# An 8192 x 8192 fp32 transpose: all stores, and all loads but the first three, issued by ScalarE instead of SyncE, with the stores ahead of the load

## The chip, the cores and the metric

One core of one Trainium2 chip. The metric is the device time of one execution, in microseconds (us), lower is better.

A ratio below is the mean time of one kernel's runs over the mean of the runs of the kernel before in the same rounds, so it is not quite the ratio of the medians quoted beside it. It comes with a 95% interval.

## The reference

```python
def setup_inputs():
    return {"x": np.random.randn(8192, 8192).astype(np.float32)}

def reference(x):
    return np.transpose(x)
```

268 MB go in and 268 MB come out; nothing is computed.

## The kernel before

The matrix is walked in 128 chunks of 128 rows by 4096 columns (2 MB). SyncE loads a chunk into one of NIN = 3 input buffers. TensorE, in a hardware loop, transposes it into the eight banks of PSUM (the memory that TensorE writes), 512 columns each. ScalarE copies the even banks and VectorE the odd banks into output registers: big buffers that gather the same bank over a window of up to 8 chunks, so that a store writes 4 KB runs. One bank closes its window in each chunk and SyncE stores that register (2 MB). There are nine registers: eight with open windows and one spare. So a window that opens in chunk t reuses the register whose store was issued in chunk t-2, and the copying engine waits for it.

```python
        def load(t):
            s, c = chunks[t]
            nc.sync.dma_start(
                out=ins[t % NIN], in_=x[c * P:(c + 1) * P, s * J:(s + 1) * J]
            ).then_inc(s_ld[t % NIN], 16)
        # ...
        for t, (s, c) in enumerate(chunks):
            closing = []
            for q in range(NR):
                e = q % 2
                eng = (nc.scalar, nc.vector)[e]
                if q not in window:
                    # ... take a register r, open a window
                    if stored[r]:
                        eng.wait_ge(s_st[r], 16 * stored[r])
                # ...
                eng.wait_ge(s_pe, t * NR + q + 1)
                # ... copy pss[q] into its place in regs[r]
            if t + NIN < T:
                nc.sync.wait_ge(s_pe, (t + 1) * NR)     # TensorE is done with chunk t
                load(t + NIN)
            for q, e, count in closing:
                nc.sync.wait_ge(s_cp[e], count)         # the last copy of the window
                # ... store regs[r] on SyncE's queue
```

Of the kernel before, what the change touches and what calls it, by code (L numbers as in the profile page):

```python
# [8 lines left out]
def physical(ap):  # L9


    t = ap.tensor
    dims = [list(d) for d in ap.ap]
    if len(dims) == 2:
        dims.insert(1, [dims[1][1], 1])
    return mybir.PhysicalAccessPattern(
        ap=dims,
        offset=ap.offset,
        dtype=ap.dtype,
        memref=t.name,  # L20
        memsetref=t.name + "_set",
    )


def wide_dma(nc, eng, queue, out, in_):


    return eng.add_instruction(
        mybir.InstDMACopy(
            mode="Copy",  # L30
            name=nc.get_next_instruction_name(),
            engine=eng.engine,
            ins=[physical(in_)],
            outs=[physical(out)],
            queue=queue,
        )
    )


@with_exitstack  # L40
def kernel(
    ctx: ExitStack,
    tc: tile.TileContext,
    x: bass.AP,
    out: bass.AP,
):






    nc = tc.nc
    P = 128
    N, M = x.shape
    assert x.shape == out.shape[::-1]
    dt = x.dtype

    S = 32
    B = 4  # L60
    W = 8
    NR = S // B
    NIN = 3
    NREG = 9
    CH = N // P
    J = S * P

    with tc.tile_critical():  # L68
        nc.alloc_sbuf_tensor("pad", [P, 32], dt)
        ident = nc.alloc_sbuf_tensor("ident", [P, P], dt).ap()  # L70
        ins = [nc.alloc_sbuf_tensor(f"in{k}", [P, J], dt).ap() for k in range(NIN)]
        regs = [nc.alloc_sbuf_tensor(f"reg{k}", [P, B * W * P], dt).ap() for k in range(NREG)]
        pss = [nc.alloc_psum_tensor(f"ps{k}", [P, B * P], dt).ap() for k in range(NR)]

        s_id = nc.alloc_semaphore("s_id")
        s_ld = [nc.alloc_semaphore(f"s_ld{k}") for k in range(NIN)]
        s_st = [nc.alloc_semaphore(f"s_st{k}") for k in range(NREG)]
        s_bank = [nc.alloc_semaphore(f"s_bank{q}") for q in range(NR)]
        s_pe = nc.alloc_semaphore("s_pe")
        s_cp = [nc.alloc_semaphore("s_cpa"), nc.alloc_semaphore("s_cpv")]  # L80

        nc.gpsimd.memset(ident, 0.0).then_inc(s_id, 1)  # L82
        nc.gpsimd.wait_ge(s_id, 1)
        nc.gpsimd.affine_select(  # L84
            out=ident,
            in_=ident,
            compare_op=mybir.AluOpType.not_equal,
            fill=1.0,
            base=0,
            pattern=[[-1, P]],  # L90
            channel_multiplier=1,
        ).then_inc(s_id, 1)

        chunks = [(s, c) for s in range(M // J) for c in range(CH)]

        def load(t):
            s, c = chunks[t]
            nc.sync.dma_start(
                out=ins[t % NIN], in_=x[c * P:(c + 1) * P, s * J:(s + 1) * J]
            ).then_inc(s_ld[t % NIN], 16)  # L100




        def transposes(t):
            k = t % NIN
            nc.tensor.sem_inc(s_ld[k], -16).wait_op(s_ld[k], 16, "sem-ge")
            for q in range(NR):
                if t:
                    nc.tensor.sem_inc(s_bank[q], -1).wait_op(s_bank[q], 1, "sem-ge")  # L110
                for b in range(B):
                    tr = nc.tensor.transpose(  # L112
                        pss[q][:, b * P:(b + 1) * P],
                        ins[k][:, q * B * P + b:(q + 1) * B * P - B + b + 1:B],
                        ident,
                    )
                    if b == B - 1:
                        tr.then_inc(s_pe, 1)

        T = len(chunks)  # L120
        nc.tensor.wait_ge(s_id, 2)
        for t in range(T % NIN):
            transposes(t)
        with nc.Fori(0, T // NIN, engines=[nc.tensor.engine]):
            for t in range(NIN):
                transposes(T % NIN + t)

        for t in range(NIN):
            load(t)

        copied = [0, 0]
        free = list(range(NREG))
        stored = [0] * NREG
        window = {}
        stores = 0

        def closes(w, t):
            t0, r, parts = w
            return t + 1 == t0 + sum(z - a for _, a, z in parts)
# [10 lines that stand above are left out]
                    span = (q - c) % W + 1  # L150
                    r = free.pop(0)
                    parts = [(s, c, min(c + span, CH))]
                    if c + span > CH and t + span < T:
                        parts.append((s + 1, 0, c + span - CH))
                    window[q] = (t, r, parts)
                    if stored[r]:
                        eng.wait_ge(s_st[r], 16 * stored[r])
                t0, r, parts = window[q]
                k = [p[0] for p in parts].index(s)
                base = B * P * sum(z - a for _, a, z in parts[:k])  # L160
                _, a, z = parts[k]
                view = regs[r][:, base:base + B * (z - a) * P].rearrange("p (b i) -> p b i", b=B)
                o = view[:, :, (c - a) * P:(c - a + 1) * P]
                i = pss[q].rearrange("p (b i) -> p b i", b=B)
                eng.wait_ge(s_pe, t * NR + q + 1)
                if e == 0:
                    cp = nc.scalar.copy(out=o, in_=i)  # L167
                else:
                    cp = nc.vector.tensor_copy(out=o, in_=i)  # L169
                if closes(window[q], t):  # L170
                    cp.then_inc(s_cp[e], 1)
                    copied[e] += 1
                    closing.append((q, e, copied[e]))
                    eng.wait_ge(s_cp[e], copied[e])
                    eng.sem_inc(s_bank[q], 1)
                else:
                    cp.then_inc(s_bank[q], 1)
            if t + NIN < T:
                nc.sync.wait_ge(s_pe, (t + 1) * NR)
                load(t + NIN)  # L180
            for q, e, count in closing:
                t0, r, parts = window.pop(q)
                nc.sync.wait_ge(s_cp[e], count)
                base = 0
                for s_, a, z in parts:
                    rows = (z - a) * P
                    j0 = s_ * J + q * B * P
                    dst = out[j0:j0 + B * P, a * P:a * P + rows]
                    dst = dst.rearrange("(q b) i -> q b i", q=P)
                    src = regs[r][:, base:base + B * rows]  # L190
                    base += B * rows
                    if stores:
                        st = wide_dma(nc, nc.sync, "qSPDynamicHW", dst, src)
                    else:
                        st = nc.sync.dma_start(
                            out=dst, in_=src.rearrange("q (b i) -> q b i", b=B)
                        )
                    st.then_inc(s_st[r], 16)
                    stores += 1
                    stored[r] += 1  # L200
                free.append(r)
        for r in range(NREG):
            nc.sync.wait_ge(s_st[r], 16 * stored[r])

# [29 lines left out]
```

## Time and profile before

| | |
|---|---|
| time, median of 3 | 1267.63 us (1267.36 to 1267.84) |
| span in the profile | 1264.3 us |
| moved | 536.89 MB in the one queue, 99.8% of the span |
| TensorE / VectorE / ScalarE busy | 718.0 / 330.8 / 278.2 us |
| load, full store: issue to landing | 19.5 us, 24.3 us |

The page's lines and their reading are in the prediction. In all such lines PE is TensorE, DVE VectorE and ACT ScalarE; SPq and ACTq are issues of transfers by SyncE and by ScalarE, and "landing" is the moment when a transfer is complete. One more view, the waits (engine, line, what it waited for: total us, times, longest):

```profile
ACT reg L167 <- DMA out_dram<-reg: 787.7, 63, 17.7
DVE reg L169 <- DMA out_dram<-reg: 746.3, 63, 17.0
```

Together 1534.0 us of standing until a store has landed.

### The profile page before, as it was taken

To read this page: it belongs to the slowest core of one execution; us is meant where nothing else is said; L and a number is where in the kernel's file an instruction comes from. 1 tells how busy PE (TensorE), PEld (TensorE's weight loads), DVE (VectorE), ACT (ScalarE), POOL (GpSimd) and SP (SyncE) were. 2 spreads that over 40 slices of the span, in tenths; PEclk is the share of its full clock that TensorE was granted. 3 is DMA by queue.
4 is the path that set the end of the run, shared out by engine and by line. 5 is a ranking of instruction groups with operands and counts; after the bars stand their busy time and mean duration, and the time that the engine had idled before them with its cause. 6 is when DMAs were issued, how large, how long until landed. Compare 5 with 4: busy or idle time off the path is not lost. (4 is left out here: it accounts for less than half of the span.)

```text
span 1264.3 us, 11043 instructions
## 1 busy us (share of the span) xinstructions
PE 718.0 (57%) x4096; PEld 679.5 (54%) x4096; DVE 330.8 (26%) x512; ACT 278.2 (22%) x513; POOL 0.7 (0%) x6
## 2 busy tenths in 40 slices
PE   5746566465565646655565564655647555565560
PEld 5646466454555546555564554655546555465550
DVE  3312213222232222221222212222122222232220
ACT  2322132121321212213122121221312213122130
POOL 0000000000000000000000000000000000000000
PEclk9977867787876877767678777887777868778785
DMA  9999999999999999999999999999999999999997
GB/s 384 428 429 429 429 429 429 429 430 429 429 430 429 429 430 430 430 430 429 430 423 417 431 430 429 430 428 431 430 428 429 430 430 431 428 429 430 429 429 308
DMA packets 39277, 537.00 MB, mean 425 GB/s; under 512 B 4320, under 2 KB 4832, under 8 KB 6240
## 3 DMA queue, kind: packets, MB, share of 16 engines
q1 hardware_dynamic: 39264, 536.89, 99.8%
q14 instruction: 12, 0.10, 0.0%
q8 instruction: 1, 0.02, 0.0%
HBM read 268.44 MB, written 268.44 MB: 425 GB/s over the span
## 5 line engine op out<-in xcount | busy, mean ns | idle before, releaser
L112 PE MATMUL ps<-ident,in 128*128 128x128 f32 x4096 | 718.0, 351 | 516.0 <-PEq L110 506.9
L112 PEld LDWEIGHTS ps<-ident,in 128*128 128x128 f32 x4096 | 679.5, 218 | 554.1 <-issue 552.9
L169 DVE COPY reg<-ps 128x512 f32<-128x512 f32 x512 | 330.8, 686 | 904.5 <-DMA out_dram<-reg 746.3
L167 ACT COPY reg<-ps 128x512 f32<-128x512 f32 x512 | 276.9, 596 | 957.4 <-DMA out_dram<-reg 787.7
L167 ACT ACT_TABLE_LOAD x1 | 1.3, 1283 | 0.9 <-SPq L68 0.9
L84 POOL TENSOR_SCALAR_AFFINE_SELECT ident<-ident 128x128 f32<-128x128 f32 x1 | 0.3, 292 | 0.2 <-POOL ident L82 0.2
L82 POOL MEMSET ident<- 128x128 f32 x1 | 0.2, 205 | 0.5 <-SPq L68 0.5
L218 POOL MEMSET const-bfloat16-1.0<- 128x1 bf16 x1 | 0.1, 101 | 0.0
L218 POOL MEMSET const-uint8-127<- 128x1 uint8 x1 | 0.1, 101 | 0.0
L218 POOL MEMSET const-float32-0.0<- 128x1 f32 x1 | 0.1, 98 | 0.2 <-issue 0.2
L218 POOL MEMSET const-float32-1.0<- 128x1 f32 x1 | 0.1, 98 | 0.0
## 6 DMA issues: line engine op xcount, KB each, us to landing
in<-in_x_dram SPq DMA_DIRECT2D x128, 2048.0 KB, 19.5
out_dram<-reg SPq DMA_DIRECT2D x114, 2048.0 KB, 24.3
out_dram<-reg SPq DMA_DIRECT2D x4, 1792.0 KB, 22.6
out_dram<-reg SPq DMA_DIRECT2D x4, 1536.0 KB, 21.3
out_dram<-reg SPq DMA_DIRECT2D x4, 1280.0 KB, 18.1
out_dram<-reg SPq DMA_DIRECT2D x4, 1024.0 KB, 19.1
out_dram<-reg SPq DMA_DIRECT2D x4, 768.0 KB, 18.8
out_dram<-reg SPq DMA_DIRECT2D x4, 512.0 KB, 17.2
```

The costliest lines, as they stand in the source:

```text
L82: nc.gpsimd.memset(ident, 0.0).then_inc(s_id, 1)
L84: nc.gpsimd.affine_select(out=ident, in_=ident, compare_op=mybir.AluOpType.not_equal, fill=1.0, base=0, pattern=[[-1, P]], channel_multipl ...
L112: tr = nc.tensor.transpose(pss[q][:, b * P:(b + 1) * P], ins[k][:, q * B * P + b:(q + 1) * B * P - B + b + 1:B], ident,)
L167: cp = nc.scalar.copy(out=o, in_=i)
L169: cp = nc.vector.tensor_copy(out=o, in_=i)
L218: nc = _bacc.Bacc("TRN2", target_bir_lowering=False, num_devices=1)
```

## The change

The intent is to free SyncE of nearly its whole program. ScalarE issues all stores and all loads but the first three, on its own queue. With it the order changes: the stores of a chunk go out from inside the row of ScalarE's copies, the load after the last copy. TensorE's loop is the same in both kernels.

```diff
-            nc.sync.dma_start(
+            (nc.sync if t < NIN else nc.scalar).dma_start(
                 out=ins[t % NIN], in_=x[c * P:(c + 1) * P, s * J:(s + 1) * J]
...
+        def store(q, e, count):
+            t0, r, parts = window.pop(q)
+            nc.scalar.wait_ge(s_cp[e], count)
...
+                    st = wide_dma(nc, nc.scalar, "qActDynamicHW", dst, src)
...
+                before = []
+                if e == 0:
+                    before, closing = closing, []
                 if closes(window[q], t):
...
+                for k in before:
+                    store(*k)
+            for k in closing:
+                store(*k)
             if t + NIN < T:
-                nc.sync.wait_ge(s_pe, (t + 1) * NR)
+                nc.scalar.wait_ge(s_pe, (t + 1) * NR)
                 load(t + NIN)
-            for q, e, count in closing:
...
-                    st = wide_dma(nc, nc.sync, "qSPDynamicHW", dst, src)
```

More of the change, by code (lines that the diff above doesn't have):

```diff
@@ L134 @@
         window = {}
-        stores = 0
+        def store(q, e, count):
+            t0, r, parts = window.pop(q)
+            nc.scalar.wait_ge(s_cp[e], count)
+            base = 0
+            for s, a, z in parts:
+                rows = (z - a) * P
+                j0 = s * J + q * B * P
+                dst = out[j0:j0 + B * P, a * P:a * P + rows]
+                dst = dst.rearrange("(q b) i -> q b i", q=P)
+                src = regs[r][:, base:base + B * rows]
+                base += B * rows
+                if any(stored):
+                    st = wide_dma(nc, nc.scalar, "qActDynamicHW", dst, src)
+                else:
+                    st = nc.scalar.dma_start(
+                        out=dst, in_=src.rearrange("q (b i) -> q b i", b=B)
+                    )
+                st.then_inc(s_st[r], 16)
+                stored[r] += 1
+            free.append(r)
         def closes(w, t):
@@ L177 @@
                     cp.then_inc(s_bank[q], 1)
+                for k in before:
+                    store(*k)
+            for k in closing:
+                store(*k)
             if t + NIN < T:
-                nc.sync.wait_ge(s_pe, (t + 1) * NR)
+                nc.scalar.wait_ge(s_pe, (t + 1) * NR)
                 load(t + NIN)
-            for q, e, count in closing:
-                t0, r, parts = window.pop(q)
-                nc.sync.wait_ge(s_cp[e], count)
-                base = 0
-                for s_, a, z in parts:
-                    rows = (z - a) * P
-                    j0 = s_ * J + q * B * P
-                    dst = out[j0:j0 + B * P, a * P:a * P + rows]
-                    dst = dst.rearrange("(q b) i -> q b i", q=P)
-                    src = regs[r][:, base:base + B * rows]
-                    base += B * rows
-                    if stores:
-                        st = wide_dma(nc, nc.sync, "qSPDynamicHW", dst, src)
-                    else:
-                        st = nc.sync.dma_start(
-                            out=dst, in_=src.rearrange("q (b i) -> q b i", b=B)
-                        )
-                    st.then_inc(s_st[r], 16)
-                    stores += 1
-                    stored[r] += 1
-                free.append(r)
         for r in range(NREG):
```

## The prediction

> **What bounds the kernel now.** I read the page first: engines, slices, queues, groups, DMA issues.
>
> ```profile
> PE 718.0 (57%) x4096; PEld 679.5 (54%) x4096; DVE 330.8 (26%) x512; ACT 278.2 (22%) x513; POOL 0.7 (0%) x6
> ...
> DMA  9999999999999999999999999999999999999997
> GB/s 384 428 429 429 429 429 429 429 430 429 429 430 429 429 430 430 430 430 429 430 423 417 431 430 429 430 428 431 430 428 429 430 430 431 428 429 430 429 429 308
> ...
> q1 hardware_dynamic: 39264, 536.89, 99.8%
> ...
> L169 DVE COPY reg<-ps 128x512 f32<-128x512 f32 x512 | 330.8, 686 | 904.5 <-DMA out_dram<-reg 746.3
> L167 ACT COPY reg<-ps 128x512 f32<-128x512 f32 x512 | 276.9, 596 | 957.4 <-DMA out_dram<-reg 787.7
> ...
> in<-in_x_dram SPq DMA_DIRECT2D x128, 2048.0 KB, 19.5
> out_dram<-reg SPq DMA_DIRECT2D x114, 2048.0 KB, 24.3
> ```
>
> No engine is busy over 57%. One DMA queue is busy 99.8% of the span, flat at about 429.5 GB/s. ScalarE and VectorE spend most of their idle time waiting for a store to land, so the transfers lead and the engines follow. Moving 536.89 MB at 429.5 GB/s takes 1250.0 us. The span is 1264.3, and the page says where the other 14 us are: a slice is 31.6 us, the first (384) loses 31.6 x (1 - 384/429.5) = 3.3 us, the slices with 423 and 417 lose 1.4, the last (308) loses 8.9; together 13.6. The time as measured, 1267.6, is 3.3 above the span.
>
> Next the SyncE timeline, because its work is what moves. An undisturbed chunk in the middle of the run, and the stretch where stores are cut in two because a window crosses from one half of the columns to the other:
>
> ```profile
> 508.30 0.33 SPq L98 DMA_DIRECT2D in<-in_x_dram  x1
> ...
> 508.67 0.55 SPq L28 DMA_DIRECT2D out_dram<-reg  x1
> ```
>
> ```profile
> 646.23 0.89 SPq L98 DMA_DIRECT2D in<-in_x_dram  x1
> 647.16 2.55 SPq L28 DMA_DIRECT2D out_dram<-reg  x2
> 655.35 0.99 SPq L98 DMA_DIRECT2D in<-in_x_dram  x1
> 656.39 3.34 SPq L28 DMA_DIRECT2D out_dram<-reg  x2
> ...
> 672.81 3.26 SPq L98 DMA_DIRECT2D in<-in_x_dram  x1
> 676.12 2.71 SPq L28 DMA_DIRECT2D out_dram<-reg  x2
> ```
>
> A load costs its issuer 0.33 us and a store 0.55 us, while landing takes some 20 us. In the split stretch an issue can take 3.3 us: there the issuer is held back, I take it because the queue has no room. That hold is the one thing that could hurt on an engine that also copies.
>
> **What the Trainium skill says.** "DMA: Bandwidth & Descriptors", section "Issuing engines are not separate DMA queues": transfers started by the scalar, sync or gpsimd engine run on the same 16 DMA engines, and a choice of issuer saves only the sequencer's initiating time. The trace of before has one queue only, so it shows only the second half: 0.33 to 0.55 us of issue against about 20 us to landing. The same page, section "Where 436 GB/s comes from", puts the ceiling at 435.2 GB/s; this trace runs at 429.5, 1.3% below, so a different issuer has nothing left to win there. "Perfetto Trace Analysis", section "DMA Instruction — HWDGE (DVE, Sync)": the record of such an instruction covers waiting for the generator, generating descriptors and excess semaphore increments, then the sequencer is free. The 0.33 us for a 2 MB load, which needs 4.9 us at 429.5 GB/s, agrees.
>
> **The change part by part.** A period is one chunk: 2 MB in and 2 MB out, 2 x 2.097/0.4295 = 9.77 us; call it P, and one transfer 4.88.
>
> Removed: SyncE's 125 later loads, 142 stores and their waits. SyncE was never on the chain for long, so removing it is worth nothing by itself.
>
> Added to ScalarE: 125 x 0.33 = 41 us of loads, 142 x 0.55 = 78 us of stores. The holds: over the two medians the split stretch shows about 21 us (for example 3.26 - 0.33 for the load at 672.81), and the last seven stores, which the timeline has as one run to the end, about 16 more. Together about 156 us. With 278 us of copies ScalarE is occupied 434 us, 34% of the span, and 957 us were idle. Per ordinary chunk that is 4 x 0.60 of copies plus 0.88 of issue, 3.3 us of 9.77. Room enough; what counts is whether an issue comes too late for the queue.
>
> Moved: SyncE sent load t+3 when TensorE had finished chunk t, then store t. Now store t goes first, from inside the row of copies, and load t+3 goes after ScalarE's last copy of chunk t. And ScalarE waits: the bank whose window closed in chunk t-1 opens a new window in chunk t, in the register stored at t-2, so every second chunk ScalarE stands still until store t-2 has landed, with issues behind it. Is the queue empty by then?
>
> First test the reckoning on before. With the queue always full and each load ahead of its store, put the landing of load t+3 at time 0. Load t landed at -29.3, store t-3 at -29.3 + 4.88 = -24.4, store t-2 at -14.7. TensorE needs the bank that waited for store t-3, about -23.8 with one copy, and finishes the chunk some 4 us later, near -19.7. So load t+3 should land 19.7 us after issue and store t 4.88 - 0.37 later in the queue than that, 24.2. The page has 19.5 and 24.3. The reckoning holds.
>
> Now the changed order, store t landing at 0 and load t+3 at 4.88. Load t landed at 4.88 - 29.3 = -24.4; store t-2 at -19.5. TensorE takes 718/128 = 5.6 us, from -24.4 to -18.8, no longer held by a bank (store t-3 landed at -29.3). Odd t: ScalarE stands until -19.5, then has up to four copies (2.4 us) and a store issue (0.55); store t goes out at about -18, load t+3 at about -16.5. Even t: VectorE is the one that stands; the store goes out between -22 and -18.5, the load near -18. A transfer must be in the queue 4.88 before it lands, so the spare time is at least 18 - 4.88 = 13 us for stores, and 16.5 + 4.88 - 4.88 = 16.5 us for loads. Before it was 24.3 - 4.88 = 19.4 and 19.5 - 4.88 = 14.6. The smallest margin falls from 14.6 to 13 us: still over two transfers. Nothing of ScalarE's added 156 us is on the path.
>
> Start: loads 0 to 2 stay on SyncE. Load 3 was issued near 14.8 us; now it follows the copy that ends at 14.94 and, with the wait, goes near 15.1. The first three loads keep the queue until about 2 + 3 x 4.88 = 16.6, so 0.3 us later costs nothing. The 256 KB first store goes out some 3 us sooner, but beside loads that fill the queue: 0. Middle: ScalarE held for up to 6 us per chunk plus 2.4 of copies is 8.4 of 9.77, and it is held only while the queue is full. End: in the last chunk ScalarE's copy of bank 6 waits for a store until 1235.82; the stores of banks 0 to 3 go out earlier either way, the later ones queue behind them. The last 8 stores are 36/8 x 2.097 = 9.4 MB, 22 us of queue: 0.
>
> Sum: 0 removed from the path, 0 added, with an error of about 1 us at each end. 1267.6 + 0 gives **1267.5 us**.
>
> **The rivals.** (1) The joined engine starves the queue: one program now has to do copies, waits for landed stores, and issues in a fixed order. For it: 787.7 us of store waits now stand ahead of loads, up to 17.7 us once, and a wait for store t-2 in front of load t+3 is a new dependence. Against it: 13 us of margin, and the queue idles only after all of it is gone. If my phase is wrong by a whole transfer, there are still 8 us. If it did bite in every second chunk by 1 us, that is 64 us: 1330. (2) The holds at a full queue stop the copies in the split stretch and at the end, then banks come free late, and TensorE falls behind. For it: issues of 2.5 to 3.4 us. Against it: full queue means transfers in hand. If it bites anyway it is some 8 chunks at 2 us and the tail at 3: 1267 + 19 = 1286. (3) It gets better: stores that enter sooner and a SyncE without a program shorten start or tail. The losses at both ends are 3.3 and 8.9 us; half the first, 1 to 2 us, is all I would credit: 1265. A gain over 2% needs 25 us, above the 435.2 ceiling for all practical purposes (536.89/0.4352 = 1234 with no ends at all).
>
> **Range and chances.** The repeats lie within 0.5 us, so the width comes from the rivals: a little of (3) below, a little of (1) or (2) above. 1263 to 1274 should hold it 8 times in 10. Faster by over 2%: 1%; within 2%: 94%; slower: 5%, nearly all of it rival (1).
>
> **What would show it.** Right: the DMA row stays at 9s and 429 GB/s; the load's time to landing grows from 19.5 to 21-23 and the full store's falls from 24.3 to 18-22, by the reckoning above; ScalarE's copies stay near 277 us; issues on its queue keep medians of 0.33 and 0.55 us. Wrong: slices under 420 GB/s in the steady part together with times to landing below 10 us (rival 1); the same in slices 20 to 22 or the last only, with issues of several us on ScalarE (rival 2). An issue that costs ScalarE well over 1 us would break the sum, and a changed plateau with no gap in the queue would be a cause I have not thought of.

## The result

The changed kernel took 1265.87 us (median of 6, 1263.30 to 1267.10) beside 1267.59 for the kernel before: ratio 0.9985, interval 0.9972 to 0.9998. That is the same at the 2% mark, and 1.6 us from the predicted 1267.5.

The page of the changed kernel: transfer engines' busy tenths and rate in 40 slices, ScalarE's queue (packets, MB, share), the two copies (busy us, mean ns, idle us and what ended most of it), and the transfers (size, us to landing):

```profile
DMA  9999999999999999999999999999999999999998
GB/s 381 426 427 429 425 430 431 428 429 431 429 429 431 429 429 430 429 430 431 426 428 411 429 429 429 430 431 429 429 431 428 430 430 429 429 429 430 430 429 355
...
q10 hardware_dynamic: 38832, 530.60, 98.9%
...
L189 DVE COPY reg<-ps 128x512 f32<-128x512 f32 x512 | 348.1, 690 | 887.2 <-PE ps L112 733.5
L187 ACT COPY reg<-ps 128x512 f32<-128x512 f32 x512 | 292.9, 588 | 941.5 <-PE ps L112 746.2
...
in<-in_x_dram ACTq DMA_DIRECT2D x125, 2048.0 KB, 22.8
out_dram<-reg ACTq DMA_DIRECT2D x114, 2048.0 KB, 19.4
```

The plateau is the same 429 GB/s, on another queue (q10). The two times to landing have changed places: load 19.5 to 22.8 us, full store 24.3 to 19.4. And the engines' waits have changed their names:

```profile
ACT reg L187 <- PE ps L112: 746.2, 384, 7.3
DVE reg L189 <- PE ps L112: 733.5, 400, 10.4
...
ACT reg L187 <- DMA out_dram<-reg: 192.5, 45, 9.1
DVE reg L189 <- DMA out_dram<-reg: 153.3, 39, 8.3
```

Waiting for landed stores has fallen from 1534.0 to 345.8 us, 1188 us less, and the time has moved by 2. The copying engines are as idle as before (941.5 and 887.2 us against 957.4 and 904.5). They now wait for TensorE, which waits for the load: the same transfer rate under another name. (The view of TensorE's own waits names L110, the wait for a bank; but all 125 idle stretches of TensorE over 1 us end 0.1 to 0.3 us after a load has landed.)

What the issues look like on ScalarE where a window crosses the two halves of the columns and stores come in pairs (start us, duration us, engine):

```profile
625.56 0.59 ACT L187 COPY reg<-ps 128x512 f32<-128x512 f32 x1
625.67 0.66 ACTq L28 DMA_DIRECT2D out_dram<-reg  x1
626.37 1.07 ACT L187 COPY reg<-ps 128x512 f32<-128x512 f32 x2 [0.21 <-issue]
626.98 5.16 ACTq L98 DMA_DIRECT2D in<-in_x_dram  x1
632.18 0.59 ACT L187 COPY reg<-ps 128x512 f32<-128x512 f32 x1 [4.73 <-PE ps L112]
```

The load is held for 5.16 us and ScalarE's next copy starts 0.04 us after the hold ends. (The page puts that copy's idle time down to TensorE, whose semaphore came last; but TensorE began that chunk at 630.16, and its first bank is copied 1.1 us after a chunk begins where nothing holds ScalarE.) The hold is real, and longer than any single load hold on SyncE before (3.41 us). It comes with the order: SyncE with the stores first (below) had one of 6.25 us. The first two lines show something kinder: the copy at 625.56 is still running when the store's issue starts at 625.67, so issuing and copying overlap unless the issue is held.

### The profile page after: what moved, and what is told of

It reads as the page before. It is cut to its first block, busy times and chain, and to the rows that moved or that the text cites. A ratio compares the mean times of both kernels' runs of the same rounds, so it can differ in the third digit from the quotient of the medians.

```text
span 1261.5 us, 11043 instructions
## 1 busy us (share of the span) xinstructions
PE 744.9 (59%) x4096; PEld 724.6 (57%) x4096; DVE 348.1 (28%) x512; ACT 294.1 (23%) x513; POOL 0.7 (0%) x6
## 5 line engine op out<-in xcount | busy, mean ns | idle before, releaser
L112 PE MATMUL ps<-ident,in 128*128 128x128 f32 x4096 | 744.9, 364 | 489.8 <-PEq L110 481.4
L112 PEld LDWEIGHTS ps<-ident,in 128*128 128x128 f32 x4096 | 724.6, 219 | 509.9 <-issue 509.9
L189 DVE COPY reg<-ps 128x512 f32<-128x512 f32 x512 | 348.1, 690 | 887.2 <-PE ps L112 733.5
L187 ACT COPY reg<-ps 128x512 f32<-128x512 f32 x512 | 292.9, 588 | 941.5 <-PE ps L112 746.2
## 6 DMA issues: line engine op xcount, KB each, us to landing
in<-in_x_dram ACTq DMA_DIRECT2D x125, 2048.0 KB, 22.8
out_dram<-reg ACTq DMA_DIRECT2D x114, 2048.0 KB, 19.4
```

Source lines behind the costliest of these rows:

```text
L112: tr = nc.tensor.transpose(pss[q][:, b * P:(b + 1) * P], ins[k][:, q * B * P + b:(q + 1) * B * P - B + b + 1:B], ident,)
L187: cp = nc.scalar.copy(out=o, in_=i)
L189: cp = nc.vector.tensor_copy(out=o, in_=i)
```

## The experiments

The theory: the transfer engines set the time, and neither the issuer nor the order matters while each transfer is in the queue early enough. Rivals: (a) two effects cancel, a gain from the order and a cost of issuing from ScalarE; (b) holds at a full queue cost time; (c) ScalarE's program is near the edge. All outputs are right.

### The changed kernel again, twice

No edit.

> The changed kernel as it is, again, for a second trace and a closer ratio. If the first result (0.9985) was real: 1264 to 1267 us, ratio 0.998 to 0.9995, and the last slices again lose less than in the kernel before. If it was luck of the runs: ratio 1.000 within 0.0007.

> The changed kernel a third time, on the same chip and in the same rounds as the order alone. If its small gain is real, ratio 0.9975 to 0.9995 again.

Measured: 1264.77 us, ratio 0.9986 (0.9973 to 0.9998), and 1265.36 us, ratio 0.9987 (0.9974 to 0.9999). With the first result the gain is 0.13 to 0.15% three times. It is real, and some 1.8 us. It sits at the end: by the prediction's way of reading the last slice, before lost 8.9 us there and the three profiles of the changed kernel (355, 327 and 359 GB/s against 429.5) lost 5.5, 7.5 and 5.2.

The packet records of before (a packet is the piece of a transfer that one transfer engine moves at a time) show a part of it. The issues of its last two stores were held until 1249.45 and 1252.30 us. From 1248.8 to 1250.2 and from 1250.8 to 1253.1 us the packets in flight fell to 5 and then to 4, where 16 are usual: engines stood, 2.4 us on average over the sixteen, until about 0.8 us after each issue was through. In the same place, 24 to 8 us before the end, the three traces of the changed kernel have no such gap (one has a gap of over 1 us earlier, at 1233.5). That is about the size of the gain, but it is one profile of before, and it was not tried by itself.

### Order alone: SyncE issues, stores before the load (run twice)

```diff
-            if t + NIN < T:
-                nc.sync.wait_ge(s_pe, (t + 1) * NR)
-                load(t + NIN)
             for q, e, count in closing:
...
                 free.append(r)
+            if t + NIN < T:
+                nc.sync.wait_ge(s_pe, (t + 1) * NR)
+                load(t + NIN)
```

> Order alone: SyncE still issues everything, but the stores of a chunk before the load. Theory (the transfers lead, only the order in the queue sets who waits for what): time within 0.3% of before, 1264 to 1270 us; the load's time to landing moves from 19.5 to about 22-23 us and the full store's from 24.3 to about 19-20, as in the changed kernel; waits of ScalarE and VectorE for landed stores fall from 1534 us to some 350. Rival (two effects cancel: the order gains, the issue from ScalarE costs): clearly faster than before, 1262 us or less.

> The order alone from SyncE again, beside the changed kernel. Theory (the small gain belongs to the order, not to ScalarE): ratio 0.9980 to 0.9995, within 0.0010 of the changed kernel. If the gain belongs to ScalarE's issue: 1.000 here and 0.9986 there.

Measured: 1266.20 us, ratio 0.9993 (0.9980 to 1.0006); again 1265.27 us, ratio 0.9988 (0.9975 to 1.0001), beside 0.9987 for the changed kernel in the same rounds. Landing, in the second run:

```profile
in<-in_x_dram SPq DMA_DIRECT2D x128, 2048.0 KB, 22.8
out_dram<-reg SPq DMA_DIRECT2D x114, 2048.0 KB, 19.7
```

SyncE with the new order has the changed kernel's times to landing and, as near as five runs tell, its time; its waits for landed stores are 193.3 + 155.1 = 348.4 us against 345.8. So the visible rearrangement of the profile is the order's doing, not ScalarE's. For whom the last 0.1% is, is less sure. Both intervals of the order alone just include 1; its ten runs together lie some 1.3 us below the kernel before (an estimate from the times), so the gain probably goes with the order. Of its two profiles, one lost 8.2 us in the last slice (318 GB/s, with a gap like that of before, of 1.0 us), nearly as much as before, and the other 5.4 (356, without the gap).

### Issuer alone: ScalarE issues, the load first, all at the end of its chunk

```diff
-                before = []
-                if e == 0:
-                    before, closing = closing, []
...
-                for k in before:
-                    store(*k)
-            for k in closing:
-                store(*k)
             if t + NIN < T:
                 nc.scalar.wait_ge(s_pe, (t + 1) * NR)
                 load(t + NIN)
+            for k in closing:
+                store(*k)
```

> Issuer alone: ScalarE issues, but the load first and the stores after it, at the end of its chunk. Theory: within 0.3% of before, although the spare time is less: with the load landing at 0, store t-2 lands at -14.7, and in odd chunks ScalarE stands until then and has up to four copies left, so those loads go out at -12.3 to -14 (landing 12 to 14 us after issue) and those of even chunks near -19; median landing of loads 14 to 17 us, of full stores 18 to 22. Spare 12.3 - 4.9 = 7.4 us, so no gap. Rival (two effects cancel): clearly slower than before, over 1272 us.

Measured: 1271.45 us (1269.47 to 1278.63), ratio 1.0043 (1.0021 to 1.0064). Slower, by less than the rival wanted and more than the theory allowed. Landing came as reckoned: loads 15.9 us, full stores 20.5. But the rate is no longer flat:

```profile
GB/s 387 429 428 427 429 429 429 430 429 429 431 430 430 429 430 430 429 429 431 426 428 416 430 429 430 429 429 430 429 430 430 429 413 406 403 415 425 429 418 318
```

Slices 33 to 36 (413, 406, 403, 415) lie under the plateau. The packet records say how: from 1050 to 1100 us 118 of 1222 packets of 16 KB took over 700 ns, in the kernel before 1 of 1310, where the ordinary one takes 611. And near the end, counting how many packets were in flight at an instant (16 engines, about one each), from the packet records:

```
us      1239.3 1239.8 1240.3 1240.8 1241.3 1241.8 1242.8 1243.3 1244.3 1244.8
packets     16     11      9      8      4      3      2      1      1     16
```

For 4.5 us, ever more engines have nothing to do while the last still works off its share. The sixteen engines do not march together.

These are two different losses. Standing engines cost 3.5 us at this end, where the kernel before lost 2.4 in its own, and over the whole run they cost no more than there. What the run lost is in the longer packets: the page has packets in 98.6 + 1.2 = 99.8% of the time of the sixteen engines, as in the kernel before, so from before to this run the packets' time grew from 1261.8 to 1268.5 us, 6.7 us, and the span by the same 6.7. The engines were busy and moved less. Why a packet takes longer when transfers are issued later is not shown. My reading is that the engines in front come to the end of the queued work first, so that the 7.4 us of spare time reckoned for the transfer as a whole are not all there for them; no run tried it.

### The moment of issue without ScalarE

Was that ScalarE's issue, or only its lateness? SyncE issues everything here, load first, but waits until ScalarE has passed its last copy of the chunk.

```diff
+                if q == 6:
+                    nc.scalar.sem_inc(s_late, 1)
...
+                nc.sync.wait_ge(s_late, t + 1)
                 nc.sync.wait_ge(s_pe, (t + 1) * NR)
                 load(t + NIN)
```

> Separates the issuer from the moment of issue. The kernel before, SyncE issues everything and the load first, but SyncE now waits for ScalarE to have passed its last copy of the chunk, so its loads go out as late as in e2_scalar_load_first (issuer alone, 1271.45 us). Theory (only the moment counts): 1269 to 1276 us, ratio 1.002 to 1.007, load landing near 16 us, full store near 20.5. Rival (issue from ScalarE itself costs): as the kernel before, 1266 to 1268 us.

Measured: 1273.85 us (1269.32 to 1279.07), ratio 1.0054 (1.0037 to 1.0072); the loads landed after 15.2 us and the full stores after 20.5 (in the profile, which is of the fastest run). With the issuer put back and the lateness kept, the cost is the same as above. So the 0.4 to 0.5% belong to the moment of issue, and issuing from ScalarE as such costs nothing that these runs can see. Rival (a) falls in its literal form, with a remainder: moving the issues to ScalarE in the old order would have cost some 5 us, because ScalarE stands still for a landed store ahead of the load. The change of order avoids that.

### Two queues: loads from SyncE, stores from ScalarE

```diff
-            (nc.sync if t < NIN else nc.scalar).dma_start(
+            nc.sync.dma_start(
...
-                nc.scalar.wait_ge(s_pe, (t + 1) * NR)
+                nc.sync.wait_ge(s_pe, (t + 1) * NR)
```

> Loads from SyncE, stores from ScalarE: two queues. Theory: the same transfer engines, so 1262 to 1272 us; loads and stores then share the engines at once, so the times to landing settle by themselves, near 15 to 25 us. If a held issue at a full queue costs anything (rival 2 of the prediction), two queues have room for more transfers and the holds of several us in the split stretch vanish, with a gain of 2 to 5 us; if they cost nothing, no gain.

Measured: 1273.81 us (1267.97 to 1279.55), ratio 1.0061 (1.0036 to 1.0086). The median is above the stated range. The times to landing, 20.3 us for loads and 19.7 for full stores, were as expected. No load's issue took over 1 us any more and 6 stores' did, against 6 loads and 7 stores in the changed kernel; the slices with split stores read 424 and 422 against 428 and 411. So room in the queues is there, and the sum got worse: late slices of 409, 421 and 399 GB/s. The profile is of one of the two quickest runs (1268.11 us), so most of the loss is not in it. Why two queues vary so from run to run I did not pursue; the loss is shown, its cause is open.

### The holds at the end

Odd banks of the last chunk are stored from SyncE's idle queue.

```diff
+            last = t0 + sum(z - a for _, a, z in parts) == T and q % 2 == 1
+            by, ring = (nc.sync, "qSPDynamicHW") if last else (nc.scalar, "qActDynamicHW")
-            nc.scalar.wait_ge(s_cp[e], count)
+            by.wait_ge(s_cp[e], count)
...
-                    st = wide_dma(nc, nc.scalar, "qActDynamicHW", dst, src)
+                    st = wide_dma(nc, by, ring, dst, src)
```

> The changed kernel, but in the last chunk the stores of the odd banks go from SyncE on its own queue, so a full queue holds no issue back at the end. Theory (the end is set by the transfer engine that lags most and is never idle, so holds at a full queue cost nothing): as the changed kernel, within 1 us. Rival 2 of the prediction (holds at the end cost something): 2 to 4 us faster than the changed kernel.

Measured: 1265.51 us (ratio 0.9995, 0.9982 to 1.0008; one of five runs at 1269.59), the changed kernel in the same rounds 1265.36. ScalarE's last issues:

```profile
1233.83 0.55 ACTq L28 DMA_DIRECT2D out_dram<-reg  x1
...
1235.54 0.55 ACTq L28 DMA_DIRECT2D out_dram<-reg  x1
...
1236.88 2.03 ACTq L28 DMA_DIRECT2D out_dram<-reg  x2
```

In the changed kernel the last four stores occupied ScalarE for 13.04 us from 1236.61. The holds on ScalarE are gone (no store's issue in the last chunk took over 1.4 us) and nothing is won. Rival (b) falls for the end of the changed kernel; in the kernel before, as shown above, engines did stand beside held issues. That the lagging engine sets the end fits the packet records (in this run 4 of 16 still work at 1257.3 us, one at 1261.3) but was not tried by itself.

### More work on ScalarE

One, and then two, useless copies inside the scratch memory before each of ScalarE's copies; ScalarE waits for each.

```diff
+                    for _ in range(1):        # 2 in e4_pad2
+                        nc.scalar.copy(out=junk, in_=junk).then_inc(s_junk, 1)   # 128x1024
+                        pads += 1
+                        nc.scalar.wait_ge(s_junk, pads)
                     cp = nc.scalar.copy(out=o, in_=i)
```

> The changed kernel with one useless copy of 128x1024 inside the scratch memory before each of ScalarE's copies, waited for by ScalarE. An estimate from ScalarE's 0.59 us for 512 elements: about 1.1 us each, so a chunk takes ScalarE 4 x 1.7 = 6.9 us plus issues, of 9.77. Theory (13 us of spare time, ScalarE not on the path): same time, 1263 to 1269 us; the load's time to landing falls from 22.8 to 17-20, since the issue is later. Rival (ScalarE's program is near the edge and each us of it counts): some 4 us per chunk of which at least a quarter shows, 1390 us or more.

> Two such copies: 4 x 2.85 = 11.4 us per chunk, over the 9.77 of the transfers. Theory: now ScalarE is the bound, 128 x 11.4 to 12 = 1460 to 1540 us, and the queue runs dry: GB/s falls in all slices to about 360, landing of loads under 10 us. This shows what starving looks like and that the room of the chunk, not the issue, is the limit. If the time stays near 1267, my estimate of ScalarE's occupation is wrong.

Measured, one: 1268.23 us (1267.73 to 1275.51), ratio 1.0028 (0.9997 to 1.0058). A pad took 1047 ns; ScalarE was busy 818.7 us instead of 294.1. So 525 us more work on the issuing engine cost 1 to 4 us against the kernel before (median and mean of ratio differ, through one run of 1275.51), and 3 to 5 against the changed kernel by its own ratio of 0.9986 (it did not run in these rounds); part of it at the start, where the second slice fell to 406 from 426 GB/s. The load's landing was reckoned at 17 to 20 us and was 21.1; the store's fell to 16.9. Rival (c), 1390 or more, falls.

Measured, two: 1467.09 us in the one run. Here is an engine that starves the queue:

```profile
DMA  7689898998999999899998999989999899998987
GB/s 286 269 319 415 343 390 363 362 418 341 399 362 366 383 368 403 356 374 382 360 390 335 354 384 361 410 339 389 375 361 414 344 392 367 360 419 342 398 356 315
...
L193 ACT COPY junk<-junk 128x1024 f32<-128x1024 f32 x1024 | 1072.0, 1047 | 84.1 <-issue 35.3
...
out_dram<-reg ACTq DMA_DIRECT2D x114, 2048.0 KB, 7.6
```

Its timeline has a store's issue at 600.90 and the next at 612.21, a chunk of 11.31 us, and 128 x 11.31 = 1448. ScalarE is 91% busy and the slices are ragged. The load's landing was expected under 10 us and was 11.8; the store's was 7.6. (TensorE's granted clock was 0.51 in this run, against 0.75 in the changed kernel, but TensorE was busy for only 68% of the span.) Between one pad and two lies the transfers' 9.77 us per chunk.

### Two input buffers instead of three

With a buffer less, every load can go out only a chunk later. NIN = 2 in both kernels, with the first two chunks taken out of the loop so that the first banks need no wait.

```diff
-    NIN = 3
+    NIN = 2
...
-        for t in range(T % NIN):
+        PRE = T % NIN or NIN
+        for t in range(PRE):
             transposes(t)
-        with nc.Fori(0, T // NIN, engines=[nc.tensor.engine]):
+        with nc.Fori(0, (T - PRE) // NIN, engines=[nc.tensor.engine]):
             for t in range(NIN):
-                transposes(T % NIN + t)
+                transposes(PRE + t)
```

> The kernel before with two input buffers instead of three. Reckoning with the load landing at 0: load t landed at -19.5, TensorE is done with the chunk at -13.9, so the next load into its buffer goes out near -13.9 and has 9 us to spare; stores go out near -13, landing 18 us later. Theory: same time within 0.5%, 1262 to 1274 us, load landing 13 to 15 us.

> The changed kernel with two input buffers. Store landing at 0: load t landed at -14.7, TensorE done at -9.1, ScalarE sends the store near -9 at the latest and the load near -8.5. The store then has 9 - 4.9 = 4 us to spare and the load 8. Theory of the margins: the changed order has less to spare than the old one here (4 against 9 us), so it is the one to suffer first; within 2% still, but 0 to 1.5% slower than the kernel before with two buffers: 1267 to 1286 us. If the order made no difference to the spare time, both would be equal.

Measured, before: 1275.87 us, ratio 1.0068 (1.0051 to 1.0085), a little over the range; loads landed after 13.6 us, as reckoned. Most of the loss is at the start: its first two slices (31.8 us each) read 329 and 383 GB/s against 384 and 428, (55 + 45)/429.5 x 31.8 = 7.4 us.

Measured, after: 1325.65 us, ratio 1.0458 (1.0422 to 1.0495). The range was 1267 to 1286, so the direction was right and the size far off.

```profile
GB/s 320 372 408 427 413 430 399 398 397 382 426 416 415 403 392 430 399 407 424 389 423 412 414 407 386 429 397 408 417 393 427 399 407 414 395 412 396 405 425 373
...
in<-in_x_dram ACTq DMA_DIRECT2D x126, 2048.0 KB, 13.8
out_dram<-reg ACTq DMA_DIRECT2D x114, 2048.0 KB, 9.9
```

The rate is ragged through the whole run. As in the load-first run from ScalarE, most of it is longer packets: by the pages' shares (99.2% of 1326.9 us against 99.8% of 1264.3) the packets' time grew by 54.5 of the 62.6 us, and engines stood for the other 8. The store's landing of 9.9 us leaves 9.9 - 4.88 = 5.0 us of spare time, about the 4 that I reckoned, but a positive margin of that size is no margin. This pair also shows a difference between the kernels that their times hide: with the same buffer taken away, one is 0.7% slower than the kernel before and the other 4.6%.

### The runs by spare time

Spare time is the smaller of the two median times to landing, less the 4.88 us of one transfer:

| run | load, store landing us | spare us | ratio to before |
|---|---|---|---|
| before | 19.5, 24.3 | 14.6 | 1 |
| changed | 22.8, 19.4 | 14.5 | 0.9985 to 0.9987 |
| e1 and e12, order alone from SyncE | 22.8 to 22.9, 19.7 | 14.8 | 0.9993, 0.9988 |
| e9, last stores on two queues | 22.7, 19.5 | 14.6 | 0.9995 |
| e4_pad1 | 21.1, 16.9 | 12.0 | 1.0028 |
| e2, load first from ScalarE | 15.9, 20.5 | 11.0 | 1.0043 |
| e10, late load from SyncE | 15.2, 20.5 | 10.3 | 1.0054 |
| e5, before with two buffers | 13.6, 18.1 | 8.7 | 1.0068 |
| e6, changed with two buffers | 13.8, 9.9 | 5.0 | 1.0458 |

e4_pad2 is left out, because ScalarE itself bounds it. The two-queue run is left out too, because the reckoning assumes one queue; reckoned so, it would have 14.8 us and, with 1.0061, break the order. But for the first four, which are level, the order of the spare times is the order of the ratios, whichever engine issues. Three reservations: the interval of e4_pad1 includes 1, most of what e5 lost it lost at the start, and the times to landing are measured in the same runs as the loss. So the table shows what goes together; what lengthens the packets stays open.

One other thing could not be tried: a tenth output register, meant to shorten the stand before the load, does not build beside three input buffers (800 bytes of each partition short). No version was measurably faster than the changed kernel.

## Why the prediction was right

The time, 1265.87 against 1267.5, lies inside 1263 to 1274, and the steps held.

- **The transfers bound.** The plateau stayed at 429 GB/s on the new queue, and a fourfold cut of the store waits moved the time by 0.15%.
- **The reckoning of phases.** It said 21 to 23 us for loads and 18 to 22 for full stores; the page says 22.8 and 19.4. The two orders have nearly the same smallest spare time, 14.6 and 14.5 us as measured (from medians), where I had 14.6 and 13 (for the worst chunks). The runs with the order alone show the same landings from SyncE.
- **Nothing of ScalarE's issues is on the path.** Two runs bear it out: adding 525 us of copies to ScalarE cost 3 to 5 us, under 1% of what was added, and putting the issuer back to SyncE at the same late moment changed nothing that the intervals show.
- **Rival 1, starving.** ScalarE can starve the queue, as two pads show, but 9.77 us per chunk leave room for one more copy of this kind at each place. I had said that the queue idles only after all of the margin is gone, and that if the phase were wrong by a whole transfer there would still be 8 us left and no loss. That part was too easy: e5, with 8.7 us left, lost 0.7%, 7.4 us of it at the start, and e2 lost 0.4% at 11. And the loss need not be idle time: in e2 and e6 most of it is packets that take longer on busy engines.
- **Rival 2, holds.** They came, up to 5.61 us on a load. The prediction had said that an issue of well over 1 us would break its sum; it did not. In the changed kernel the holds cost nothing that shows: the two slices with split stores lost 1.5 us (428 and 411 GB/s) against 1.4 before, and without holds at the end nothing changed. The reason given, that a held issue means a full queue and transfers in hand, does not hold for every engine: at the end of the kernel before, an issue was held while only 4 of 16 packets were in flight.
- **Rival 3, a small gain.** I credited 1 to 2 us to start and tail; 1.8 us came, in the profiles from the tail and not from the start (first slice 384 and then 381). That it goes with the order is likely (0.9993 and 0.9988 for the order alone), not certain. The gap beside the last two held stores of before, 2.4 us, would account for it; that was not tried.

Three sizes were off without harm. The issue of a load was to keep its median of 0.33 us and has 0.60: where it follows straight after a store's issue (64 of 125 loads; 46 from SyncE in the same order) and is not held, it takes 0.59 to 0.94, alone mostly 0.34. All issues on ScalarE sum to 89.5 + 92.7 = 182 us, not 156; SyncE with the same order has 91.7 + 93.7 = 185, so this too is the order. And ScalarE's copies were to stay near 277 us and have 292.9. They are no slower (588 ns mean against 596). In before they came in rows after each landed store, five in 2.54 us, now mostly one at a time, 0.59 each. The Trainium skill, "ScalarE: Activation LUTs", section "What ACT_TABLE_LOAD costs", says that back-to-back activations overlap by about 93 ns; the trace comes near it for copies: (5 x 0.586 - 2.54)/4 = 98 ns.

## What to carry to other kernels

Where one transfer queue is busy throughout, ask of each issue only how long before its turn it enters the queue: write down which landing releases it, and check the reckoning on the kernel you have, by the times to landing, before you trust it for the change. Large waits that vanish from a page are no gain if the same idle time comes back under another name. Keep the spare time well over one transfer (here 11 us, over two transfers, already went with a loss of 0.4%), and look for what stands ahead of an issue in the new engine's program: here the move cost 0.4% in the old order and nothing in the new.

## What the Trainium skill lacked or had wrong

- "DMA: Bandwidth & Descriptors", section "Issuing engines are not separate DMA queues", says that all issuers run on the same 16 engines and that several issuers save only sequencer time. For one queue moved to another issuer the runs agree (0.9987 from ScalarE, 0.9988 from SyncE in the same order). It does not say that two issuers at once can be slower: loads and stores on separate queues took 1.0061 of the time, with runs from 1267.97 to 1279.55 us.
- No page that I read gives a figure for how early an issue must come. For 2 MB transfers of 4.88 us each in one queue, the runs with 14.5 us of spare time lost nothing, the one with 11 us lost 0.4%, the one with 5 us 4.6%. Nor does one say that busy transfer engines can then move less: 118 of 1222 packets of 16 KB took over 700 ns in one stretch of the run with 11 us, where 611 is usual.
- "DMA: Bandwidth & Descriptors", section "Why a DMA increments its semaphore by 16 and not by 1", says that the engines of one transfer finish independently, but no page that I read says how far apart: with one queue for all, the packets in flight fell from 16 to 11, 4 and 1 within 4.5 us before the next issue filled them again (e2_scalar_load_first, 1239.3, 1239.8, 1241.3 and 1243.3 us).
- "Perfetto Trace Analysis", section "DMA Instruction — HWDGE (DVE, Sync)", counts lock wait, generation and semaphore writes in the record of an issue. It does not give a size for an issue held back with much already queued: 5.16 us for one load here, against 0.34 when free, and ScalarE's next copy started only 0.04 us after it.
